# The four dedicated tiles of the first mixer's output weights, used in reverse order of their places in memory

## The chip, the cores and the metric

The kernel runs on one core of one Trainium2 chip. The metric is the device time of one execution in microseconds (us); less is better. Three runs of the kernel before gave 2841.07, 2842.59 and 2849.51 us; the median is 2842.59 us.

## The reference, cut to what matters

The program is one inference step of a two-layer decoder on 1024 prompt tokens, 16 meta tokens and 8 x 8 sample tokens, 1104 columns in all. The first layer is an mLSTM mixer with 8 heads, the second an attention with forget gates; each is followed by a SwiGLU block. The part that matters here is the end of the first mixer and its output product with `w_out` (1024 x 1024):

```python
def mlstm_mixer(xn, C0, n0, m0, lead, w_in, b_ig, b_fg, mh_g, w_out):
    p = xn @ w_in
    ...
    h, state = mlstm_sequence(q, k, v, li, lf, state0, lead)
    h = rmsnorm(h.transpose(0, 2, 1, 3), mh_g)
    out = (h.reshape(B, T, HV).astype(xn.dtype) * jax.nn.sigmoid(og)) @ w_out
    return out, state
...
h = h + a
h = h + swiglu(rmsnorm(h, prm['norm_ffn'][l]), prm['w_gate_up'][l], prm['w_down'][l])
```

## The kernel before, in words

Activations lie feature by token: 8 blocks of 128 features by 1104 columns. A product is made of three matmuls per block, since each float32 operand is split into a high and a low part: `mm3` (lines 192 to 195) multiplies weight high by activation high (L193), weight high by activation low (L194) and weight low by activation high (L195).

**The mLSTM layer** (`phase_a`, `recurrence`). The recurrence walks over 9 chunks of tokens. Between its steps it runs the projection of the output gates (PSUM tile `mmA`, lines 193 to 195), whose sigmoids (`stg`, L765) GpSimd stores to DRAM (`ogD`, L766), and the normalised heads: `gate_head` loads a gate back (L781, tiles `ogqk`, `ogeb`, later `ogc`), transposes one head of the state output `vA` on TensorE (`ghps`, L1360), multiplies (L1361) and splits into `xh` and `xl` (L267, L268), the input of the output product. The weights of the output product were split earlier and lie in DRAM as eight pairs `woD[0]` to `woD[7]`, each a high and a low half of 512 KB.

**The output product** (`mlp`, l = 0, where `heads` is set). The result is made in units `unit(t, m, x)`: 276 columns t by 128 output features m, 24 matmuls into a PSUM tile `pops` (4 buffers), then an add into the residual `vA` on VectorE (L531) and a square on ScalarE. The first eight units are t = 0 with m = 0 to 7 in this order; TensorE's order is written by hand there, and heads of the recurrence that are left are gated between the units, one after each of m = 1 to 3 and 5 to 7, two after m = 4. The columns t = 3 run with m = 4, 5, 6, 7, 0, 1, 2, 3.

Each m needs its own pair of weights, high and low. Four pairs go to tiles of a pool of their own (`wo2`, shown as `wo` in the profile, numbered 308 to 311 in the order of allocation), the other four to the tiles `slots` 2 to 9 (`held`). All sixteen halves are loaded by SyncE's queue in the order m = 0 to 7, high then low, at L508:

```python
for m in range(KT):
    for z in range(2):
        nc.sync.dma_start(ws[m][z].bitcast(F32), self.woD[m][:, z])
```

The pool of the `wo2` tiles is opened after the pools of the recurrence are closed, so its four tiles lie on memory that tiles of the first layer held, and a load into one of them waits for the last use of what lay there. SyncE's queue takes its instructions in order: a load that waits holds all behind it. What lay under the four differs. Under 308 and 309 were, among others, the `stg` tiles whose last store is the one of L766; under 310 and 311 the weight pool of the gates' projection (`wraw`, `whi`, `wlo`), whose last reader is the projection's last matmul (`mmA`, L195).

Of the kernel before, what the change touches and what calls it, by code (L numbers as in the profile page):

```python
# [176 lines left out]
class Net:  # L177
# [292 lines left out]
    def mlp(self, H, raws, w, l, heads=None, cb=None):  # L470
# [5 lines left out]
        with self.pool(self.uid("nsp")) as sp, self.pool(self.uid("npp"), bufs=2, space=PSUM) as pn:  # L476
# [14 lines left out]
            with ExitStack() as c:  # L491
# [5 lines left out]
                ws = []  # L497
                for _ in range(4):
                    w2 = wp.tile([P, 2, KT, P], F32R, name=self.uid("wo2"))
                    ws.append((w2[:, 0], w2[:, 1]))  # L500
                held = [(cut(slots[a]), cut(slots[b])) for a, b in (
                    ((2, 6), (3, 7), (4, 8), (5, 9)) if heads else ((4, 5), (8, 9), (2, 6), (3, 7)))]
                ws = ws + held if heads else held + ws
                raws_open = ExitStack()
                if heads:
                    for m in range(KT):
# [2338 lines left out]
```

## Time and profile before

| what | value |
|---|---|
| median of three runs | 2842.59 us |
| the profiled execution, its own time | 2839.24 us |
| its span, first to last instruction | 2837.5 us |
| mean granted TensorE clock | 0.997 of full speed |
| TensorE busy, whole span | 2764.9 us |
| first use of a `wo` tile in a matmul | 437.30 us from the span's start |

All places are given in us from the span's start. A timeline row has start, duration, engine, line, operation, output and input, and in brackets the idle time of the engine just before it and what ended it. A row of waits has the waiting engine and line, the releaser, and then total us, times and longest. PE is TensorE, PEld its weight load, DVE VectorE, ACT ScalarE, POOL GpSimd, SP SyncE; SPq is SyncE's queue of DMA issues. In the rows on DMA, q1 is the queue that SyncE fills and q0 the one that GpSimd fills.

### The profile page before, as it was taken

Reading aid. Unit: us, or ns where it says so; the run is one execution under the profiler, and the core shown is the slowest. Engines: PE = TensorE matmul, PEld = TensorE weight load, DVE = VectorE, ACT = ScalarE, POOL = GpSimd, SP = SyncE. Lnnn points to the kernel's source line nnn. Section 1 sums busy time; section 2 is a strip of 40 time slices with the busy share of each in tenths; the row PEclk is TensorE's granted clock in tenths of the full one; section 3 lists DMA queues with packets and bytes.
Section 4 is the critical chain, followed back from the end, with each engine's and each line's share of the span. In section 5 each row is a group of like instructions: output and inputs, shape, how many; then the busy total and the mean of one; then the engine's idle time right before and its main releaser. Section 6 shows DMA issues by size and latency. Waiting matters only on the chain. (4 is left out here: it accounts for less than half of the span.)

```text
span 2837.5 us, 60524 instructions
## 1 busy us (share of the span) xinstructions
PE 2764.9 (97%) x23614; PEld 2651.7 (93%) x23614; DVE 1772.9 (62%) x3921; ACT 1166.4 (41%) x2279; POOL 830.9 (29%) x1307
## 2 busy tenths in 40 slices
PE   7999998999999999999999999999999999999998
PEld 7999888999999999999999888677999999999998
DVE  5142566788888655573355443777478888765656
ACT  5232363333233233454344445877443323323345
POOL 3022233223223222224353202454312322323111
PEclk9999999999999999999999999999999999999999
DMA  6374537245555365644453686342524555526556
GB/s 193 113 207 136 146 107 273 81 130 168 176 168 160 111 211 187 201 155 153 145 173 136 218 302 231 129 168 88 156 76 135 168 176 169 161 90 231 183 193 214
DMA packets 428393, 469.45 MB, mean 165 GB/s; under 512 B 40030, under 2 KB 354522, under 8 KB 427082
## 3 DMA queue, kind: packets, MB, share of 16 engines
q1 hardware_dynamic: 378978, 316.78, 35.8%
q0 software_dynamic: 43600, 143.14, 15.2%
q10 hardware_dynamic: 5528, 5.65, 0.6%
q8 instruction: 186, 3.05, 0.4%
q14 instruction: 101, 0.83, 0.1%
HBM read 318.25 MB, written 147.21 MB: 164 GB/s over the span
## 5 line engine op out<-in xcount | busy, mean ns | idle before, releaser
L1416 PE MATMUL m<-xh,slot 128*128 128x276 f32 x2752 | 540.6, 290 | 1.8 <-ACT fs L1445 1.8
L1416 PEld LDWEIGHTS m<-xh,slot 128*128 128x128 f32 x2752 | 439.6, 188 | 3.7 <-ACT fs L1445 2.2
L1416 PE MATMUL m<-xl,slot 128*128 128x276 f32 x1376 | 397.1, 289 | 0.0
L1416 PEld LDWEIGHTS m<-xl,slot 128*128 128x128 f32 x1376 | 258.7, 188 | 0.0
L193 PE MATMUL tmps<-slot,xh 128*128 128x256 f32 (+2 forms) x864 | 243.1, 281 | 0.0
L195 PE MATMUL tmps<-slot,xl 128*128 128x256 f32 (+2 forms) x864 | 240.6, 278 | 0.0
L194 PE MATMUL tmps<-slot,xh 128*128 128x256 f32 (+2 forms) x864 | 240.5, 278 | 0.0
L268 DVE TENSOR_TENSOR slot<-slot,slot 128x1024 fp32r<-128x1024 f32 x124 | 162.7, 1313 | 59.4 <-ACT slot L267 57.9
L267 ACT CAST slot<-slot 128x1024 fp32r<-128x1024 f32 x124 | 129.5, 1045 | 141.4 <-PE m L1416 109.9
L194 PEld LDWEIGHTS tmps<-slot,xh 128*128 128x128 f32 (+1 forms) x864 | 159.2, 184 | 0.1
L195 PEld LDWEIGHTS tmps<-slot,xl 128*128 128x128 f32 (+1 forms) x864 | 158.6, 184 | 0.0
L193 PEld LDWEIGHTS tmps<-slot,xh 128*128 128x128 f32 (+1 forms) x864 | 158.4, 183 | 0.2
L193 PE MATMUL mmA<-xh,whi 128*128 128x384 f32 (+1 forms) x384 | 134.3, 350 | 0.1
L194 PE MATMUL mmA<-xl,whi 128*128 128x384 f32 (+1 forms) x384 | 127.4, 332 | 0.0
L195 PE MATMUL mmA<-xh,wlo 128*128 128x384 f32 (+1 forms) x384 | 127.2, 331 | 0.0
L268 DVE TENSOR_TENSOR slot<-vA,slot 128x1024 fp32r<-128x1024 f32 (+1 forms) x59 | 82.3, 1397 | 32.7 <-ACT slot L267 31.5
L268 DVE TENSOR_TENSOR slot<-Ht,slot 128x1024 fp32r<-128x1024 f32 (+1 forms) x59 | 82.0, 1393 | 32.8 <-ACT slot L267 31.6
L256 DVE TENSOR_TENSOR wlo<-wraw,whi 128x1024 fp32r<-128x1024 f32 (+1 forms) x32 | 39.0, 1225 | 101.0 <-ACT whi L255 78.0
L267 ACT CAST slot<-Ht 128x1024 fp32r<-128x1024 f32 (+1 forms) x59 | 60.9, 1037 | 95.5 <-PE m L1416 88.5
L267 ACT CAST slot<-vA 128x1024 fp32r<-128x1024 f32 (+1 forms) x59 | 60.8, 1035 | 95.4 <-PE m L1416 86.5
L1520 DVE TENSOR_TENSOR ws<-ws 128x128 f32<-128x128 f32 x264 | 93.8, 355 | 8.9
L2667 ACT ACTIVATE s<-s,nb 128x272 f32<-128x272 f32 (+7 forms) x126 | 98.9, 787 | 0.0
(788 smaller groups left out, 8666.2 us busy)
## 6 DMA issues: line engine op xcount, KB each, us to landing
ws<-in_w_down SPq DMA_DIRECT2D x176, 128.0 KB, 2.5
sD<-ws SPq DMA_DIRECT2D x176, 128.0 KB, 2.1
slot<-sD SPq DMA_DIRECT2D x40, 512.0 KB, 5.4
slot<-in_w_gate_up SPq DMA_DIRECT2D x36, 512.0 KB, 4.1
kp<-in_cache_k SPq DMA_DIRECT2D x32, 512.0 KB, 6.2
vp<-in_cache_v SPq DMA_DIRECT2D x32, 512.0 KB, 6.7
vA<-in_w_gate_up SPq DMA_DIRECT2D x26, 512.0 KB, 4.4
Ht<-in_w_gate_up SPq DMA_DIRECT2D x26, 512.0 KB, 3.9
```

The source lines that it names most:

```text
L193: mm(ps, sh, mh, start=first, stop=False)
L194: mm(ps, sh, ml, start=False, stop=False)
L195: mm(ps, sl, mh, start=False, stop=last)
L256: low = lambda: nc.vector.tensor_tensor(out=lo, in0=raw, in1=hi.bitcast(F32), op=ALU.subtract)
L267: self.nc.scalar.copy(hi, src)
L268: self.nc.vector.tensor_tensor(out=lo, in0=src, in1=hi.bitcast(F32), op=ALU.subtract)
L1416: nc.tensor.matmul(u.ps[h, b], w[p][:, k], x[q][:, k], start=first and k == i == 0, stop=k == 3 and i == 2, skip_group_check=True)
L1520: tt(out=o, in0=a, in1=b, op=ALU.subtract)
L2667: nc.scalar.activation(ss[z, u], ss[z, u], AF.Exp, bias=nb[:, z : z + 1], accum_out=sm[:, u, z : z + 1])
```

## The change

The list of the four pairs of tiles is reversed before the weights are assigned to it. Which weight is used when, by which instruction, stays; the tiles change places: m = 0 lies in tile 311, m = 1 in 310, m = 2 in 309 and m = 3 in 308.

```diff
-                ws = ws + held if heads else held + ws
+                ws = [ws[x] for x in (3, 2, 1, 0)] + held if heads else held + ws
```

The instructions stand in the same order on every engine; what differs is the tile that they name and what they wait for.

SyncE's queue at L508, the loads of m = 0 to 3, with the semaphores that each waits for (DMAHW is a landing of SyncE's queue, DMASW one of GpSimd's, the others are engines). Before:

```order
L508 DMA wo_308_4944<-woD_1996 128x1024 [waits DMASW4_49,DMASW3_49,DMASW5_49,DMASW2_49,DMASW6_49,DMASW1_49,DMASW7_49,DMASW0_49,DMAHW3_49,Activation_49,Pool_49]
L508 DMA wo_308_4944<-woD_1996 128x1024 [waits DMAHW4_49]
L508 DMA wo_309_4945<-woD_2005 128x1024 [waits DMAHW1_49,DMAHW2_49,DMASW6_49,DMAHW5_49,DMASW1_49,DMASW0_49]
L508 DMA wo_309_4945<-woD_2005 128x1024 [waits DMAHW6_49]
L508 DMA wo_310_4946<-woD_2014 128x1024 [waits DMAHW7_49,PE_49]
L508 DMA wo_310_4946<-woD_2014 128x1024 [waits DMAHW0_49]
L508 DMA wo_311_4947<-woD_2427 128x1024 [waits PE_49]
L508 DMA wo_311_4947<-woD_2427 128x1024
```

The same place after the change:

```order
L508 DMA wo_311_4947<-woD_1996 128x1024 [waits DMASW1_49,DMASW0_49,DMASW6_49,DVE_49,DMAHW3_49,PE_49,Activation_49]
L508 DMA wo_311_4947<-woD_1996 128x1024 [waits DMAHW4_49]
L508 DMA wo_310_4946<-woD_2005 128x1024 [waits DMAHW5_49,DMAHW2_49,Activation_49]
L508 DMA wo_310_4946<-woD_2005 128x1024 [waits DMAHW6_49]
L508 DMA wo_309_4945<-woD_2014 128x1024 [waits DMASW5_49,DMASW4_49,DMASW6_49,DMASW3_49,DMASW7_49,DMASW2_49,DMAHW1_49,DMASW1_49,DMAHW7_49,DMASW0_49,Activation_49]
L508 DMA wo_309_4945<-woD_2014 128x1024 [waits DMAHW0_49]
L508 DMA wo_308_4944<-woD_2427 128x1024 [waits DMASW5_49,DMASW7_49,DMASW4_49,Pool_49]
L508 DMA wo_308_4944<-woD_2427 128x1024
```

What moved is the wait DMASW3: by its value it is for the last store of `stg` (L766). It stood ahead of the first pair and stands ahead of the third now. The first pair's latest waits are PE_49, by its value the last matmul of the gates' projection (`mmA`, L195), and landings, copies and splits that are ahead of that matmul. DVE_49 and Activation_49 there are the splits of the projection's weights. The other loads of L508, for m = 4 to 7, wait for what they waited for.

TensorE where unit (0, 0) begins. Before:

```order
L1063 MATMUL nnpP<-ident,nnP 4x128
L193 MATMUL pops_4977<-xh,wo_308_4944 128x276 [waits DMAHW3_49]
L194 MATMUL pops_4977<-xl,wo_308_4944 128x276
L195 MATMUL pops_4977<-xh,wo_308_4944 128x276 [waits DMAHW4_49]
L193 MATMUL pops_4977<-xh,wo_308_4944 128x276
```

After the change:

```order
L1063 MATMUL nnpP<-ident,nnP 4x128
L193 MATMUL pops_4977<-xh,wo_311_4947 128x276 [waits DMAHW3_49]
L194 MATMUL pops_4977<-xl,wo_311_4947 128x276
L195 MATMUL pops_4977<-xh,wo_311_4947 128x276 [waits DMAHW4_49]
L193 MATMUL pops_4977<-xh,wo_311_4947 128x276
```

Here only the tile moved; the unit still waits for the two halves of m = 0, wherever they lie, right behind the last matmul of the recurrence (L1063).

## The prediction

> **What bounds the kernel now.** I read the page first, then TensorE's waits around the first use of a `wo` tile, then the timelines of TensorE, SyncE's queue, GpSimd and VectorE there, and last the DMA queues in stretches. The page:
>
> ```profile
> span 2837.5 us, 60524 instructions
> ## 1 busy us (share of the span) xinstructions
> PE 2764.9 (97%) x23614; PEld 2651.7 (93%) x23614; DVE 1772.9 (62%) x3921; ACT 1166.4 (41%) x2279; POOL 830.9 (29%) x1307
> ```
>
> TensorE is idle for 72.6 us in all, so the end is set by its row of work, and an idle stretch there is worth about its length. TensorE's waits from 400 to 460 us hold such a stretch:
>
> ```profile
> PE pops L193 <- DMA wo<-woD: 3.8, 1, 3.8
> ...
> PE pops L195 <- DMA wo<-woD: 1.6, 1, 1.6
> ```
>
> TensorE waits for the high half of the first pair of weights, then for the low half. Its timeline shows where:
>
> ```profile
> 422.90 0.33 PE L195 MATMUL mmA<-xh,wlo 128*128 128x384 f32 x1
> ...
> 433.21 0.27 PE L1063 MATMUL nnpP<-ident,nnP 128*4 128x128 f32 x1
> 437.30 0.60 PE L193 MATMUL pops<-xh,wo 128*128 128x276 f32 x1 [3.82 <-DMA wo<-woD]
> ...
> 439.75 0.60 PE L195 MATMUL pops<-xh,wo 128*128 128x276 f32 x1 [1.62 <-DMA wo<-woD]
> ...
> 443.98 0.29 PE L193 MATMUL pops<-xh,wo 128*128 128x276 f32 x1
> ...
> 447.04 0.49 PE L1360 MATMUL ghps<-ident,vA 128*128 128x128 f32 x3
> 447.28 0.37 PE L193 MATMUL pops<-xh,wo 128*128 128x276 f32 x1
> 447.49 0.29 PE L194 MATMUL pops<-xl,wo 128*128 128x276 f32 x1
> 447.62 0.29 PE L195 MATMUL pops<-xh,wo 128*128 128x276 f32 x1
> ```
>
> The recurrence ends at 433.48; unit 0 runs from 437.30 to 443.98, unit 1 to 447.04, and unit 2 starts behind the transposes of one head at 447.28. Unit 0 takes 6.68 us, unit 1, with the same 24 matmuls, 3.06. Only 1.62 of the difference is the second wait; the rest is the clock, by the windows of one microsecond (the last three numbers are granted clock, DMA share, GB/s):
>
> ```profile
> 435.00:436.00 1.00, 0.00 (x0) 0.00 (x0) 1.00 (x4) 0.94 (x6) 0.00 (x0) 0.95 0.91 209
> 436.00:437.00 1.00, 0.00 (x0) 0.00 (x0) 0.90 (x8) 0.95 (x5) 0.84 (x2) 0.50 1.01 387
> ...
> 442.00:443.00 1.00, 1.00 (x7) 1.00 (x7) 0.40 (x1) 0.00 (x0) 0.00 (x0) 0.64 1.03 410
> 443.00:444.00 1.00, 1.00 (x10) 1.00 (x10) 0.00 (x0) 0.00 (x0) 0.00 (x0) 1.00 1.02 406
> 450.00:470.00 20.00, 20.00 (x163) 20.00 (x162) 10.79 (x20) 6.21 (x13) 9.27 (x14) 1.00 1.00 347
> 470.00:560.00 90.00, 89.96 (x721) 89.37 (x720) 64.28 (x113) 33.13 (x61) 26.75 (x37) 1.00 0.34 111
> ```
>
> The clock falls to 0.50 at about 435.9, 2.4 us after the last matmul, and is back at about 442.7. So the late weights cost 3.82 + 1.62 + (6.68 - 1.62 - 3.06 = 2.00) = **7.44 us**. The last two rows show that nothing behind takes this back: TensorE has no gap to 560.
>
> Why the weights are late stands in the timelines of SyncE's queue and of GpSimd, in SyncE's waits and in the landings:
>
> ```profile
> 430.02 4.35 SPq L508 DMA_DIRECT2D wo<-woD  x8
> 437.33 12.10 SPq L508 DMA_DIRECT2D slot<-woD  x8
> ...
> SPq L508 <- DMA ogD<-stg: 87.5, 1, 87.5
> ...
> 427.56 0.55 POOL L766 DMA_DIRECT2D ogD<-stg  x1 [2.84 <-ACT stg L765]
> 429.15 0.90 POOL L495 DMA_DIRECT2D vA<-hD  x1 [1.05 <-PE ghps L1360]
> ...
> vA<-hD POOLq DMA_DIRECT2D x1, 1104.0 KB, 9.4
> ...
> ogD<-stg POOLq DMA_DIRECT2D x1, 192.0 KB, 2.2
> ```
>
> SyncE stood for 87.5 us with nothing else to do until the last `stg` store landed (427.56 + 2.2 is 429.8), and all eight halves for the `wo` tiles were issued from 430.02 on.
>
> **The change part by part.** No instruction is added or removed, and durations stay. Two things move. First, the loads of m = 0 and 1 lose the wait for the store. Their latest wait is now the projection's last matmul, which ends at 422.90 + 0.33 = 423.23. They are issued from 423.3 on, 6.7 us earlier. The first half landed 437.30 - 430.02 = 7.3 us after its issue, the second 9.7 us, in a crowded stretch. Even at that price the first pair lands at 433.0, ahead of 433.48, so **unit 0's waits of 3.82 and 1.62 go, and with the idle stretch the half clock**. What else unit 0 needs are the `xh` and `xl` of the first heads, in VectorE's timeline with two rows that I need below:
>
> ```profile
> 431.71 0.51 DVE L268 TENSOR_TENSOR xl<-ogeb,xh 128x336 fp32r<-128x336 f32 x1 [0.54 <-ACT xh L267]
> ...
> 437.00 0.08 DVE L1271 DVE_READ_ACCUMULATOR2_ANT ssqA<- 128x1 f32 x1
> ...
> 438.91 3.50 DVE L1344 TENSOR_TENSOR vA<-vA,fA 128x1024 f32<-128x1024 f32 x3
> ```
>
> They are ready at 432.22. So unit 0 can run from 433.48 to 436.54, unit 1 to 439.60, the transposes 0.24, and unit 2 starts at 439.84.
>
> Second, m = 2 now carries the wait for the store, m = 3 stands behind it, and both are issued from 430.02 on. Here the next thing is late. Bytes that each queue moved before, q0 in 425 to 431, then q0 and q1 in 431 to 437, then q1 in 437 to 441, 441 to 444 and 444 to 450:
>
> ```profile
> q0 software_dynamic: 211, 0.64, 34.8%
> ...
> q0 software_dynamic: 247, 1.06, 58.1%
> q1 hardware_dynamic: 171, 0.63, 37.1%
> ...
> q1 hardware_dynamic: 326, 1.20, 74.0%
> ...
> q1 hardware_dynamic: 322, 1.18, 98.9%
> ...
> q1 hardware_dynamic: 548, 1.99, 84.2%
> ```
>
> SyncE's queue had moved 0.63 MB by 437, 1.83 by 441, 3.01 by 444 and 5.00 by 450; a pair is 1.05 MB. The first pair was complete at 439.75, with 0.63 + 1.20 x 2.75 / 4 = 1.45 MB moved: 0.40 MB of later halves were under way. After the change the queue has a start. Issued at 430.02, it has no row up to 431 and moved bytes from then on, 1 to 3 us later; so it now begins at about 425.3; to 431 the engines can carry 5.7 us x 0.41 MB (410 GB/s of the window at 442), that is 2.34, less q0's 0.64: about 1.65 MB moved by 431, which I take. Then pair m is complete when the old count reaches 1.05 (m + 1) + 0.40 - 1.65: for m = 2 at 1.90 MB, 441.2; m = 3 at 2.95, 443.8; m = 4 at 4.00, 447.0; m = 5 at 5.05, 450.2. Unit 2 needs its low half at its third matmul, 0.34 us behind its start, at 440.2, and **waits 1.0 us**. Unit 3 then needs its own at 444.6, unit 4 at 447.9, unit 5 at 451.4: none waits. The pairs m = 4 and 5 are issued when the `ssqA` sums (437.08) and `vA` (442.41) are done on VectorE, as before, and the queue is full until then.
>
> The bounds of this wait: nothing, if the queue shares better than I take it; and 3.6 us, if up to 431 it moves only at its rate of 431 to 437 (0.63 / 6 x 5.7 = 0.60 MB by 431; m = 2 at 2.95, 443.8, against 440.2), which at more than 2.4 us idle brings the half clock and its 2.0 back. I stay near the middle since q0 is nearly empty from 427 to 431.
>
> A rule bears on the clock. The Trainium skill, "TensorE: Matmul & The Clock Gate", part 1, says that the gate judges activity over free-running windows of about 3.4 us, and halves the clock after an idle one. The half clock here, from 435.9 to 442.7, lasts 6.8 us, two such windows, so the trace agrees; by that rule a wait of 1.0 us keeps the full clock, and the sum is the same.
>
> Behind: VectorE is busy with L1344 until 442.41, so the adds of units 0 and 1 come late. `pops` has four buffers, and unit 4 starts only at 447.5; this costs nothing. It would cost a wait of unit 4 if that cover were gone. The loads of m = 0 and 1 put 2.1 MB beside GpSimd's loads and the store between 425 and 431; the store delayed by 1 us would add up to 1 us to unit 2's wait, which lies in the bounds.
>
> **Sum**: 7.44 - 1.0 = **6.4 us** less. The profiled execution took 2839.24 us, 1.74 over its span and 3.35 under the median shown. I start from the middle of all four known executions (2839.24, 2841.07, 2842.59, 2849.51), that is 2841.8, and predict **2835.4**.
>
> **The rivals.** (a) *Unit 2 takes over the wait.* The pessimistic share above: 7.44 - 3.6 - 2.0 = 1.8 us gained, 2840.0. For it: between 431 and 437 SyncE's queue got only 0.63 of 1.69 MB. Against it: q0 has little to move up to 431.
>
> (b) *The store is starved.* The early 2.1 MB hold back the store at 427.56, on which m = 2, and behind it all of SyncE's queue, now waits. If it lands only after `vA<-hD`, which was 9.4 us under way from 429.15, at 438.5, then m = 2 is complete 9.7 us later, at 448.2. TensorE idles from 439.8, goes cold (2.0), and unit 2's third matmul, at 447.62 before, is 0.6 us later and the clock costs 2.0: **2.6 us slower**, 2844.4. This decides against the change once the store lands later than 435.9 (435.9 + 9.7 + 2.0 = 447.6). Against it: q0 and q1 both moved bytes in every stretch from 431 to 444 in which both had work. A rule speaks for the danger: "DMA: Bandwidth & Descriptors", in the Trainium skill, section on issuing engines, says that transfers of all issuing engines run on the same 16 DMA engines and interleave. The same page, section on queues and rings, has each engine take turns between queues packet by packet; by that the store is slowed, not starved, which agrees with the two rows of 431 to 437.
>
> (c) *It does nothing*: the pairs land early, but the gain is lost between here and the end, 2841.8. Against it: the full rows to 560.
>
> (d) *It brings more*: no wait at unit 2, and a later wait shortened too: 7.4 plus 1 to 2, 2833.
>
> **How the numbers follow.** Forecast 0.66, (a) 0.17, (b) 0.05, (c) 0.06, (d) 0.06. The forecast's own range, with waits of 0 to 2.2 and 1.5 us of scatter between executions, is 2833 to 2838. The range to hold the time 8 times in 10 takes in (a) and (d) with scatter: 2830.5 to 2841.5. A measurement of this kernel can tell 0.3%, 8.5 us, from no change; the edges are 2834.06 and 2851.1. The forecast lies 1.3 us above the lower edge, within the scatter of executions (3.35 us among the three lowest), so two fifths of it, 0.27, and (d) count as faster: 0.33, and 0.01 of (a). Slower by 0.3% takes (b) at its worst, 0.03. The rest, 0.63, is within 0.3%.
>
> **What would show it.** SyncE's first `wo` load at 423.3 instead of 430.02, the third pair near 430 to 431; no wait of `pops` L193 at unit 0, which starts near 433.5; granted clock 1.00 from 433 to 445; a wait of about 1 us at the third matmul of unit 2, near 440; unit 3 near 444. It is wrong if the first pair is issued later than 424, if unit 2 or 3 waits for more than 2.4 us, or if the clock falls to 0.50 there. A gain at 450 us that is not found at the end speaks for (c).

## The result and the profile after

| kernel | median us | lowest to highest | runs |
|---|---|---|---|
| before | 2843.03 | 2841.07 to 2849.51 | 6 |
| changed | 2834.35 | 2832.82 to 2837.3 | 6 |

The ratio is 0.9968, with a 95% interval from 0.9955 to 0.9981: 8.7 us less, by the interval 5.4 to 12.8 us. The forecast was 2835.4 us, its range 2830.5 to 2841.5.

The page of the changed kernel:

```profile
span 2835.5 us, 60526 instructions
PE 2769.2 (98%) x23614; PEld 2656.7 (94%) x23614; DVE 1772.6 (63%) x3921; ACT 1167.3 (41%) x2279; POOL 831.1 (29%) x1307
```

As many matmuls as before (23614), in a shorter span. The span shrank by 2.0 us only, while the medians differ by 8.7, so single executions must be compared place by place. I use one point that every trace has: **E**, the end of the recurrence's last matmul (L1063, 433.48 before). All starts of units below count from E. What the expectations call the end of the output product is the first matmul of its last unit, the 32nd. TensorE of the changed kernel:

```profile
424.93 0.34 PE L195 MATMUL mmA<-xh,wlo 128*128 128x384 f32 x1
...
435.24 0.27 PE L1063 MATMUL nnpP<-ident,nnP 128*4 128x128 f32 x1
435.27 0.38 PE L193 MATMUL pops<-xh,wo 128*128 128x276 f32 x1
...
441.72 0.37 PE L193 MATMUL pops<-xh,wo 128*128 128x276 f32 x1
441.93 0.28 PE L194 MATMUL pops<-xl,wo 128*128 128x276 f32 x1
442.36 0.40 PE L195 MATMUL pops<-xh,wo 128*128 128x276 f32 x1
...
445.51 0.37 PE L193 MATMUL pops<-xh,wo 128*128 128x276 f32 x1
...
446.11 0.39 PE L195 MATMUL pops<-xh,wo 128*128 128x276 f32 x1
...
540.22 0.29 PE L193 MATMUL pops<-xh,wo 128*128 128x276 f32 x1
```

In this execution E is 435.24 + 0.27 = 435.51, 2.03 us later than in the execution of before. The change has no part in that: the first loads that it moves go out behind the projection's last matmul, that matmul ends 2.04 us later as well (425.27 against 423.23), and from its end to E it is 10.24 us here and 10.25 before. Unit 0 now starts at E - 0.24 (before, E + 3.82), unit 2 at E + 6.21 (before, 13.80), and the last unit at 540.22 - 435.51 = E + 104.71. Before, the last unit stood at 544.66:

```profile
544.66 0.29 PE L193 MATMUL pops<-xh,wo 128*128 128x276 f32 x1
```

That is E + 111.18. So the product gained **6.47 us** from E on. What lies behind, to the end of the span, took 2837.5 - 544.66 = 2292.8 us before and 2835.5 - 540.22 = 2295.3 after; 6.47 - 2.03 - 2.4 is the 2.0 of the two spans. Over all traces of this study that rest lies between 2292 and 2299 us, with no order by kernel.

SyncE's queue in the changed kernel, and what its loads waited for:

```profile
425.33 11.98 SPq L508 DMA_DIRECT2D wo<-woD  x8
439.26 8.04 SPq L508 DMA_DIRECT2D slot<-woD  x8
```

```profile
SPq L508 <- PE mmA L195: 37.5, 1, 37.5
...
SPq L508 <- DMA ogD<-stg: 7.5, 1, 7.5
```

The first load goes out 0.06 us after the projection's last matmul (424.93 + 0.34), by the clock of the execution before at 423.3. In place of the one wait of 87.5 us the queue has one of 37.5 us for that matmul, behind 43.4 us for an earlier landing, and one of 7.5 us for the store, which now stands in the middle of the eight issues (they stretch over 11.98 us, before over 4.35). The store itself, in GpSimd's timeline, and its landing:

```profile
429.59 0.55 POOL L766 DMA_DIRECT2D ogD<-stg  x1 [2.84 <-ACT stg L765]
```

```profile
ogD<-stg POOLq DMA_DIRECT2D x1, 192.0 KB, 5.4
```

It took 5.4 us to land, 2.2 before: the third pair was issued at about 429.59 + 5.4 = 435.0, not 2.2 us behind the store. From 425 to 435 SyncE's queue had moved 0.95 + 0.64 + 0.48 = 2.07 MB, nearly all of the first two pairs. From 435 to 437 it moved 0.02 MB, while GpSimd's queue took the engines with 0.73 MB. TensorE's loads of weights show what that cost, and the windows that no half clock came of it:

```profile
PEld pops L195 <- DMA wo<-woD: 0.7, 2, 0.4
PEld pops L195 <- DMA slot<-woD: 0.2, 1, 0.2
```

```profile
433.00:436.00 3.00, 2.88 (x25) 2.61 (x26) 1.88 (x7) 1.23 (x4) 0.37 (x1) 1.00 1.04 409
436.00:450.00 14.00, 13.76 (x106) 13.12 (x105) 11.19 (x31) 6.44 (x18) 4.39 (x8) 1.00 1.03 397
450.00:470.00 20.00, 20.00 (x166) 20.00 (x166) 9.98 (x19) 6.36 (x14) 9.76 (x15) 1.00 0.98 332
470.00:560.00 90.00, 89.96 (x717) 89.38 (x716) 67.16 (x117) 33.30 (x61) 25.28 (x35) 1.00 0.34 108
```

The waits are at the third matmuls (the first use of a low half) of units 2, 3 and 4. Unit 2's third matmul begins 0.64 us behind its first, where it was 0.34 before, unit 3's 0.60. The steps from unit 2 to 3, 3 to 4 and 4 to 5 took 3.79, 3.76 and 3.94 us against 3.39, 3.36 and 3.68 before: 1.06 us in all. At the start of unit 2 the gain was 13.80 - 6.21 = 7.59; less 1.06 it is 6.5.

### The profile page after: what moved, and what is told of

Same layout as the page of the kernel before. It is cut to its first block, busy times and chain, and to the rows that moved or that the text cites. A ratio compares the mean times of both kernels' runs of the same rounds, so it can differ in the third digit from the quotient of the medians.

```text
span 2835.5 us, 60526 instructions
## 1 busy us (share of the span) xinstructions
PE 2769.2 (98%) x23614; PEld 2656.7 (94%) x23614; DVE 1772.6 (63%) x3921; ACT 1167.3 (41%) x2279; POOL 831.1 (29%) x1307
## 3 DMA queue, kind: packets, MB, share of 16 engines
q8 instruction: 186, 3.05, 0.4%
## 5 line engine op out<-in xcount | busy, mean ns | idle before, releaser
L195 PE MATMUL tmps<-slot,xl 128*128 128x256 f32 (+2 forms) x864 | 240.9, 279 | 0.0
L195 PEld LDWEIGHTS tmps<-slot,xl 128*128 128x128 f32 (+1 forms) x864 | 158.7, 184 | 0.0
L195 PE MATMUL mmA<-xh,wlo 128*128 128x384 f32 (+1 forms) x384 | 127.2, 331 | 0.0
```

What stands on the lines that cost most here:

```text
L195: mm(ps, sl, mh, start=False, stop=last)
```

## The experiments

The theory: the gain comes from the two first pairs no longer standing behind the store, so it hangs on what lay under their tiles, on both pairs, and on the loads of the pairs used first. Rivals: the reverse order itself counts; bytes moved early count, for whichever weight; it is the clock alone that counts; the queue's head alone counts. There were eleven runs, two of them of the changed kernel and two of the same other order. All edits are against the kernel before, and every row gives medians of this kernel and of the kernel before on the same chip:

| run | this us | before us | ratio and interval | unit 0, 1, 2 from E | last unit from E |
|---|---|---|---|---|---|
| before | | | | 3.82, 10.50, 13.80 | 111.18 |
| changed | 2834.35 | 2843.03 | 0.9968 [0.9955, 0.9981] | -0.24, 2.91, 6.21 | 104.71 |
| e5, changed again | 2836.35 | 2843.94 | 0.998 [0.997, 0.999] | -0.24, 2.89, 6.20 | 108.13 |
| e11, changed again | 2834.9 | 2843.44 | 0.9968 [0.9956, 0.998] | -0.35, 3.47, 6.77 | 104.22 |
| e1, first pair only | 2838.41 | 2843.27 | 0.9982 [0.9973, 0.9991] | -0.24, 4.53, 10.36 | 107.75 |
| e2, other bytes early | 2843.35 | 2843.27 | 1.0003 [0.9994, 1.0012] | 5.13, 10.61, 13.90 | 111.27 |
| e8, first tile kept | 2844.12 | 2843.94 | 1.0005 [0.9997, 1.0014] | 4.00, 10.66, 13.96 | 111.44 |
| e3, 30 more matmuls | 2843.0 | 2843.27 | 1.0 [0.9991, 1.0009] | 4.01, 10.65, 13.96 | 111.42 |
| e7, 50 more matmuls | 2843.91 | 2843.94 | 1.0002 [0.9992, 1.0011] | 6.28, 9.34, 12.65 | 110.13 |
| e4, other two first | 2837.82 | 2843.27 | 0.9984 [0.9974, 0.9994] | -0.34, 3.46, 6.75 | 104.16 |
| e6, the same again | 2838.18 | 2843.94 | 0.9979 [0.997, 0.9988] | -0.35, 3.52, 6.84 | 104.37 |
| e9, stores elsewhere | 2842.32 | 2843.44 | 0.9998 [0.999, 1.0007] | -0.25, 2.88, 6.17 | 103.60 |
| e10, the same, no pad | 2837.72 | 2843.44 | 0.998 [0.9972, 0.9989] | -0.25, 2.88, 6.17 | 104.15 |

E isn't quite the same point in all of these. From the end of the projection's last matmul to E it is 10.24 to 10.26 us in most traces, but 11.23 in e11, 11.20 in e4, 11.18 in e6, 11.77 in e7, 11.60 in e9 and 11.70 in e10. In these six the clock falls to half ahead of E, between 432.6 and 435.9. Counted from there, the last unit stands at 121.43 before, 114.95 in the changed kernel, 118.38 in e5, 115.45 in e11, 115.36 in e4 and 115.55 in e6: gains of 6.48, 3.05, 5.98, 6.07 and 5.88 us.

### e1: only the first pair on free memory

Only m = 0 gets tile 311; m = 1 gets 308 and so still waits for the store.

```diff
-                ws = ws + held if heads else held + ws
+                ws = [ws[x] for x in (3, 0, 1, 2)] + held if heads else held + ws
```

> Order of tiles 311, 308, 309, 310: only m = 0 is free of the wait for the store, m = 1 carries it. E is the end of the recurrence's last matmul (L1063), 433.48 before. Theory (each pair is worth what its own wait costs): unit 0 starts at E + 0.1 with no wait; the second pair is issued about 3.5 us ahead of E, as the first pair before, and is complete near E + 6.3, so unit 1 waits about 3 us in its first matmuls; unit 2's third matmul comes near E + 9.6 (E + 14.1 before, E + 6.9 changed) if the clock holds, up to 2 us later if it falls. That is 3 to 4.5 us less than before, 4 us more than the changed kernel. Rival (only the first pair counts): as the changed kernel, E + 6.9.

TensorE's waits from 432 to 460 us:

```profile
PE pops L193 <- DMA wo<-woD: 1.5, 1, 1.5
...
PE pops L195 <- DMA wo<-woD: 0.7, 1, 0.7
```

Unit 0 starts as early as in the changed kernel, then unit 1 waits 1.5 us for its high and 0.7 us for its low half, and the clock is at half from 441.4 for 3.41 us. The local gain is 111.18 - 107.75 = 3.4 us, the times say 4.9. **Both pairs count**: the first gives half, and with it alone the next unit takes over a part of the wait and of the half clock.

### e2: the two free tiles loaded first, with the weights that are used third and fourth

The tiles stay as before; the loads of m = 2 and 3, whose tiles are free early, go ahead.

```diff
-                    for m in range(KT):
+                    for m in (2, 3, 0, 1, 4, 5, 6, 7):
```

> Tiles as before, but the queue loads m = 2 and 3 (tiles 310 and 311) first, then 0 and 1: the same bytes are moved early as in the changed kernel, for other weights. Theory (the wait at unit 0 decides): two pairs are issued at the projection's last matmul, the pair of unit 0 only at the store, so unit 0 waits as before or up to 1.5 us longer; 0 to 1.5 us slower than before, granted clock 0.50 again. Rival (the gain is relief of a crowded DMA stretch, whoever moves early): at least 4 us less than before.

SyncE's queue issues as early as in the changed kernel, and TensorE waits as before:

```profile
425.54 12.21 SPq L508 DMA_DIRECT2D wo<-woD  x8
```

```profile
PE pops L193 <- DMA wo<-woD: 5.1, 1, 5.1
...
PE pops L195 <- DMA wo<-woD: 0.5, 1, 0.5
```

2 MB moved 7 us sooner, and nothing gained: not the bytes count but whether they are those of the next matmul.

### e8: the first tile kept, two free ones right behind it

```diff
+                ws = [ws[x] for x in (0, 3, 2, 1)] + held if heads else held + ws
```

> Order of tiles 308, 311, 310, 309: m = 0 keeps its tile and with it the wait for the store at the head of the queue; m = 1 and 3 change theirs. Theory (the queue takes its loads in order, so a free tile behind a waiting one is worth nothing): as before, output product ended near E + 111.2, 0 us. Rival (each tile's own wait counts, whatever stands ahead in the queue): m = 1 early, 1 us or more less.

```profile
430.29 4.81 SPq L508 DMA_DIRECT2D wo<-woD  x8
```

```profile
PE pops L193 <- DMA wo<-woD: 4.0, 1, 4.0
...
PE pops L195 <- DMA wo<-woD: 1.4, 1, 1.4
```

All eight loads go out together behind the store, as before, though the second and third pair's tiles were free 6.8 us earlier. One waiting load at the head of the queue holds all that stand behind it, and the change lives from taking it off the head.

### e3 and e7: the clock by itself

Matmuls whose result nobody reads are put ahead of unit 0, so that TensorE works while the weights are on their way; the outputs stay. e3 has 30 of them, e7 50 (`range(50)`, `i == 49`).

```diff
+                if heads:
+                    ps = pp.tile([P, 512], F32, name=self.uid("warm"), tag="po")
+                    xw = self.X[0][0]
+                    for i in range(30):
+                        nc.tensor.matmul(ps[:, :SL], xw[:, i % 4, :P], xw[:, i % 4], start=i == 0, stop=i == 29)
```

> Tiles and loads as before, and 30 matmuls of 276 columns on data that is there, into a PSUM tile that nobody reads, between the recurrence and unit 0, so that TensorE is busy while it waits for the weights. Theory: the half clock is gone (1.00 from 433 to 445), the waits for the two halves end when they ended before (E + 3.8 and E + 6.3), and unit 0 takes 22 x 0.128 = 2.8 us from its third matmul instead of 4.2: 1.4 us less than before. Rival (most of the gain is the clock): 4 us less or more. Rival (the clock costs nothing here): 0.

> As the run with 30 spare matmuls, but with 50 of them, which last 6.4 us, so that TensorE is busy until both halves of the first pair have landed. Theory (30 were too few: TensorE still stood 1.8 us before the low half, and the clock fell for the window behind it): clock 1.00 from 433 to 450, unit 0 without a wait from about E + 6.4, unit 1 at E + 9.5 instead of E + 10.5, 1 us less at the end of the output product (E + 110.2), which the times can hardly show. Rival (the clock falls anyway): E + 111.2 or later.

TensorE's timeline of e3, and two stretches of its windows:

```profile
435.34 4.02 PE L556 MATMUL warm<-xh 128*128 128x276 f32 x30
439.59 0.37 PE L193 MATMUL pops<-xh,wo 128*128 128x276 f32 x1 [0.23 <-DVE fA L1341]
...
441.88 0.60 PE L195 MATMUL pops<-xh,wo 128*128 128x276 f32 x1 [1.79 <-DMA wo<-woD]
```

```profile
440.00:442.00 2.00, 0.21 (x2) 0.13 (x1) 1.46 (x3) 0.42 (x2) 0.00 (x0) 0.93 1.02 411
442.00:444.00 2.00, 2.00 (x9) 2.00 (x10) 2.00 (x3) 0.00 (x0) 1.07 (x2) 0.50 1.03 414
```

The 30 filled the wait for the high half, not the 1.79 us for the low one, and the clock fell at 441.7 all the same: I had expected it to stay up, and the trial says nothing on the price of the clock. With 50 it does:

```profile
436.59 6.80 PE L556 MATMUL warm<-xh 128*128 128x276 f32 x50
```

```profile
436.00:450.00 14.00, 14.00 (x108) 13.91 (x109) 8.37 (x26) 4.72 (x14) 2.18 (x4) 0.97 1.02 379
```

No wait for weights, and no half clock in unit 0: it takes 9.34 - 6.28 = 3.06 us, as the prediction had it for a warm unit with its weights there. But it starts 2.46 us later than before (E + 6.28 against 3.82), since the matmuls take longer than the high half is late. By the working of the prediction that is -1.62 for the second wait, -2.00 for the clock and +2.46, so 1.16 us gained; the last unit comes at E + 110.13, 1.05 us sooner. In this trace a half clock ran ahead of E already, from 433.5 to 436.9, and not because of the spare matmuls, which start at 436.59. From the projection's last matmul its last unit stands at 121.90, against 121.43 before. **The 2.0 us for the clock hold for unit 0, but keeping it up without earlier weights gives about 1 us at most**, too little to be seen in the times.

### e4 and e6: the other order of the two free tiles

m = 0 and 1 get 310 and 311, m = 2 and 3 get 308 and 309: each half of the list keeps its order. e6 is the same kernel again.

```diff
+                ws = [ws[x] for x in (2, 3, 0, 1)] + held if heads else held + ws
```

> Order of tiles 310, 311, 308, 309: not the reverse, but again the two tiles without the store's wait come first. Theory (what counts is which tiles lay under the stores): as the changed kernel, unit 2's third matmul near E + 6.9, 7 to 9 us less than before. Rival (the reverse order itself, or the place of a tile in memory, counts): 2 us or more away from the changed kernel.

> The order 310, 311, 308, 309 once more, beside the changed kernel. Theory (only which tiles lay under the stores counts; the 3.5 us between the two medians of the first runs is scatter of executions): within 2 us of the changed kernel of this call, output product ended between E + 104 and E + 105. Rival (the order of the two matters): again 3 us or more slower than the changed kernel.

The last unit is at E + 104.16 and 104.37, as in the changed kernel (104.71 and 104.22), and from the projection's last matmul at 115.36 and 115.55, as in e11 (115.45), which has the half clock ahead of E like these two: in the product the reverse order is nothing by itself. **What counts is which two tiles are used first.** The store is slowed in the same way; e4's landing:

```profile
ogD<-stg POOLq DMA_DIRECT2D x1, 192.0 KB, 6.0
```

By the times the gain of e4 is 5.5 us, less than the 7 to 9 expected. Both runs are some 3 us above two of the changed kernel's three, with intervals that overlap; beside the changed kernel on one chip (e6 and e5) the ratios are 0.9979 and 0.998. All 20 runs of this order have a median of 2838.00 us, all 21 of the changed kernel 2835.35. E was at 437.85 and 438.10 in the two traces and at 432.45 to 436.27 in the three of the changed kernel; the program up to there has the same work. Whether the 2 to 3 us between the two orders are chance is not settled.

### e5 and e11: the changed kernel again

> The changed kernel once more, on the same chip as the other runs of this call. Theory: 6.5 us less than before, which is what the first trace of it shows between the recurrence's last matmul (E) and the end of the output product (E + 111.2 before, E + 104.7 changed), and the 8.7 us between the first medians is partly scatter: 5 to 8 us. Rival (something else in the program also got shorter): 8.5 us or more again, and more than 104.7 + 0.5 is not seen locally.

> The changed kernel on the same chip as the two others of this call. Theory: units 2 and 3 wait 0.3 to 2 us for the third and fourth pair, with the half clock behind it in some executions: output product ended between E + 104.5 and E + 108.5, 4 to 9 us less than before. Rival (the wait of 1.9 us at unit 3 in the second run was a single disturbance): never more than E + 104.8, and times no wider than those of the kernel before.

e11 has no wait for a `wo` tile that the profile shows, and from E it repeats the first trace within 0.5 us, a little better than expected and as its rival had it. But it had lost 1 us ahead of E: the clock was at half from 434.0 to 437.4, unit 0 took 3.82 us in place of 3.15. Counted from the end of the projection's last matmul, the third matmuls of units 2 and 3 came 1.25 and 0.87 us later than in the first trace, which is enough to find their weights there. e5 is not like these. Its timeline of TensorE:

```profile
439.50 0.39 PE L195 MATMUL pops<-xh,wo 128*128 128x276 f32 x1 [0.35 <-DMA wo<-woD]
...
445.20 0.45 PE L195 MATMUL pops<-xh,wo 128*128 128x276 f32 x1 [1.94 <-DMA wo<-woD]
```

and its windows, cut 0.2 us behind the changes of the clock:

```profile
442.17:445.59 3.42, 1.48 (x11) 1.17 (x10) 1.93 (x4) 1.30 (x4) 1.22 (x2) 0.97 1.03 401
445.59:449.00 3.41, 3.41 (x18) 3.41 (x17) 0.82 (x2) 0.58 (x2) 1.43 (x3) 0.53 1.02 387
```

Here unit 3 waits 1.94 us for its low half, and the clock is at half for the next 3.41 us. The last unit comes at E + 108.13, so this execution kept 3.05 of the 6.5 us, less than the 5 to 8 expected of it. **In this one, the rival (a) of the prediction came true**, a unit later than it said: the same kernel, the same order, a store that landed 5.6 us after its issue, and the fourth pair arriving some 2 us later than in the first trace; why so much later is not shown. The margin behind the first two pairs is thin. The nine runs of e5's comparison lie between 2834.47 and 2842.21 us.

### e9 and e10: the stores' tiles on other memory

If the last store is the one thing that holds back the third pair, then with the `stg` tiles elsewhere all eight loads wait for the projection at most. In e9 their pool is opened behind the pool of the projection's weights, and a tile of the same size that nobody uses fills the old place; e10 has no such tile. Both keep the tiles' order of before.

```diff
-        st = c3.enter_context(self.pool("stA", bufs=3))
+        c3.enter_context(self.pool("padA")).tile([P, 3 * GL], F32, name="pad")
...
         self.wpools(c3, 2, 3, side="left")
+        st = c3.enter_context(self.pool("stA", bufs=3))
```

> Tiles in the order of before (308 to 311), but the stg tiles are allocated behind the projection's weight pool, and a pad of their size, which nobody writes, stays in their old place: no wo tile lies on memory that a store reads. Theory (only the store's wait was late): the first pair waits for the recurrence's state update (the last TENSOR_TENSOR of C on GpSimd, L1200, done at E - 14.3), the other three for the projection's last matmuls (E - 10.3) or earlier; the first four pairs have moved by about E + 1, units 0 to 3 start without any wait, and no waits of 0.3 to 2 us at units 2 and 3 as the changed kernel has them: output product ended at E + 103.7 to E + 104.3, 7 us less than before and 0.5 to 3 less than the changed kernel. The start of the program is scheduled a little differently, so its first 200 us can differ by 1 or 2 us. Rival (early loads take the DMA engines from the recurrence's own loads): E itself comes 3 us later or more, no gain over the changed kernel.

> As the run with the pad, but without the pad, so that the weight pool moves down into the place of the stg tiles. Theory: the same, except that tile 309 now waits for the projection's second last matmul: output product ended at E + 103.7 to E + 104.7. Rival: as for the run with the pad.

e9's issues at L508, all eight without a break of more than the queue's own:

```profile
426.25 5.71 SPq L508 DMA_DIRECT2D wo<-woD  x8
```

In its product nothing waits for a `wo` tile, and the last unit stands at E + 103.60, 1.1 us better than the changed kernel's trace, about the 1.06 us lost at units 2 to 4 there. But the kernel's time is that of before, since E itself comes at 441.87. Moving the pools changed what the first layer waits for; TensorE between 100 and 200 us, first in e9, then before:

```profile
100.00:200.00 100.00, 94.51 (x673) 92.49 (x672) 28.95 (x60) 23.20 (x43) 15.42 (x28) 0.95 0.31 103
```

```profile
100.00:200.00 100.00, 99.18 (x714) 97.35 (x714) 32.54 (x63) 26.80 (x51) 15.89 (x29) 0.98 0.39 123
```

TensorE did 673 matmuls there instead of 714. One wait stands out in e9, which before doesn't have:

```profile
178.27 0.69 PE L193 MATMUL mmA<-xh,whi 128*128 128x384 f32 x1 [4.14 <-ACT stg L733]
```

Ahead of that activation ScalarE had stood 8.85 us for `mA` on VectorE, where before it stood 4.8. e10 has the local gain as well (104.15), an E of 440.28 and 2837.72 us. Neither is better than the change; the expectation was right on the product and wrong on the whole, because it took the rest of the program as untouched. Its rival is true for a small part: beside the early loads VectorE waits 1.3 us (e9) and 1.4 us (e10) for a gate (`ogqk`), and E stands 11.60 and 11.70 us behind the projection's last matmul, with the half clock in it. But that matmul itself ends 7.0 and 5.4 us later than before. For e10 that was not traced further.

## Why the prediction was right, point by point

- **The price of the late weights, 7.44 us** (3.82 and 1.62 us of waits, 2.00 of half clock): right. The gain at the start of unit 2, before any new wait, is 7.59 us. e8 and e2 show that it all comes from the loads of the first pairs standing behind the store, and e1 that m = 1 is worth about as much as m = 0 (3.0 and 3.4 us). e7 bears out the split: unit 0 takes 3.06 us when its clock is full and its weights are there.
- **First load at 423.3**: right, 0.06 us behind the projection's last matmul in the changed trace. Unit 0 waits for nothing. The bytes were right too: SyncE's queue had moved 1.59 MB by 433.0, which is 431 in the clock of before, where the prediction has 1.65.
- **Third pair near 430 to 431**: wrong. Put into the clock of the execution before, it went out at 435.0 - 2.0 = 433.0. The step that failed is the store's time: the prediction held 2.2 us, with a delay by 1 us as a side case; it took 5.4, 5.4 and 5.6 us in the three traces of the changed kernel and 6.0 in e4. With one pair early it took 3.6 (e1), and with none 2.1 to 2.2 (before, e3, e7, e8), so the delay goes with the early loads. The low half of the third pair was there 7.3 us behind the store's landing, by unit 2's third matmul at 442.36; the first pair's took 9.7 before.
- **A wait of 1.0 us at unit 2**: right in size, not in place. In the first trace it is 1.06 us, spread over units 2, 3 and 4; in e11 nothing, in e5 2.3 us at units 2 and 3 and a half clock. That the size agrees has luck in it: the pair left later than I took it, but found its queue all but empty, where I had counted bytes of the first pairs.
- **Full clock from 433 to 445**: so in the first trace. In e5 the clock was at 0.50 at unit 3, which the prediction names as a sign that it is wrong, and in e11 at the start of unit 0.
- **Sum 6.4 us**: from E 6.47 and 6.96 us (e11: 111.18 - 104.22) in two traces, 3.05 in the third; from the projection's last matmul 6.48, 5.98 and 3.05. By the times it is 8.7, 7.6 and 8.5 us, with intervals that reach down to 5.4, 2.8 and 5.7. The 1.5 to 4.5 us between the two are not settled; the executions' scatter ahead of E, 432.45 to 438.10 in traces of kernels that are alike up to there, is enough for it, but that is argued, not shown.
- **The rivals.** (a), a later unit takes over the wait, held in one execution of three, at unit 3. (b), the store starved, did not decide: it was late by 3.2 us, and landed at 435.0 - 2.0 = 433.0 by the clock of before, 2.9 us ahead of the point from which it would have cost. The Trainium skill, "DMA: Bandwidth & Descriptors", section on queues and rings, has each DMA engine take turns between the queues packet by packet; that both queues moved bytes from 431 to 435 in the changed trace (1.12 MB on SyncE's, 0.53 on GpSimd's) agrees with it. The store landed only when 2.07 of the 2.10 MB had moved, so whether it was slowed throughout or held to the end of the burst isn't shown. (c), the gain lost behind, is excluded by the times. (d) would have needed the waits of units 2 to 4 to go with the clock kept up ahead of them. In e9 they are gone, and the last unit comes 1.1 us sooner from E; but a half clock runs ahead of E, and from the projection's last matmul nothing is won (115.20 against 114.95).

## What to carry to other kernels

Where a pool is opened on memory that others have just left, its tiles are not alike: each load waits for the last reader or store of what lay there, so give the tiles that were free first to the weights that are used first, and look at the head of the loading queue before anything else. Loads that go out earlier slow what runs beside them, and if one of those is a store for which a later load waits, that store's landing beside the burst has to go into the sum, not its landing alone. A gain of a few us in a kernel that scatters by as many is read from a place in the trace up to which both kernels are alike, with more than one execution of each, and that place has to lie ahead of all that the change moves and of the clock's falls around it: here the projection's last matmul serves better than E.

## What the runs showed of the hardware

The granted clock moves on a grid of 3.41 us whose phase differs between executions, and a window needn't be idle to cost the next one its clock. Windows of before, cut on that grid:

```profile
432.45:435.86 3.41, 1.03 (x12) 0.61 (x10) 2.76 (x11) 2.33 (x9) 0.00 (x0) 1.00 0.98 256
435.86:439.27 3.41, 0.83 (x2) 0.50 (x2) 2.33 (x14) 2.40 (x6) 1.10 (x2) 0.51 1.00 395
```

The first holds 1.03 us of TensorE's work, and the second runs at half. In e5 a window with some 1.5 us of work (above) did the same. In the changed kernel two windows of the recurrence's tail hold more, and the clock stays up:

```profile
428.20:431.62 3.42, 2.50 (x23) 2.02 (x23) 1.82 (x5) 1.49 (x4) 0.99 (x2) 1.00 1.00 346
431.62:435.03 3.41, 2.44 (x21) 1.95 (x22) 2.16 (x6) 1.66 (x5) 1.75 (x3) 1.00 1.03 413
```

Busy time alone doesn't decide it. Cut where the clock falls, windows with 1.65 us of work in e11 and in e4 and with 1.80 in e9 were followed by a half clock, and 1.91 us in before (429.0 to 432.5) was not; but neither was 1.77 us in e1 (263.9 to 267.3). And in before a window with 3.21 us (186.7 to 190.1), mostly matmuls of 8 columns (L949, L950), was followed by one. The Trainium skill, "TensorE: Matmul & The Clock Gate", part 1, gives the window as 3413 ns and free-running, which agrees with the grid, and has the clock fall after an idle window; here a window with 1.03 to 1.80 us of work was enough, and the measurement decides. How much work a window needs isn't settled by these runs. So the same wait can cost a half window or not: the same tail of the recurrence was followed by one in e11, and not in the first trace of the changed kernel. Where the grid falls on it is the likely reason. The executions also have windows at half clock in the first 200 us, one before (190.1 us) and three in the changed kernel's trace (21.8, 100.3 and 192.5), which is one likely reason why E isn't at the same place twice.
